# Attention heads every 13 chunks, a lead of two gate pairs, and branch tensors kept in HBM

## The chip, the core and the metric

The kernel runs on one core of a Trainium2 chip. The metric is the device time of one execution in microseconds; lower is better. Three runs of the kernel before gave 492.33, 492.91 and 493.28 us (median 492.91). The engines that matter are TensorE (PE, and PEld for its weight loads), VectorE (DVE), ScalarE (ACT), GpSimd (POOL) and SyncE (SP, which issues most transfers).

## What is computed

One decoder layer on 512 rows of 1024 columns, in float32:

```
h = rmsnorm(x) * norm_g
a_x, a_z, b_q, b_k, b_v, b_z, c_q, c_k, c_v, c_z, gates = split(h @ w_in)
ya = pool_mixer(a_x) * silu(a_z)            # causal windows of 2, 4, 8, 16 rows, then a 128x128 mix per group
yb = sliding_window_attention(b_q, b_k, b_v, sinks) * silu(b_z)    # 8 heads of 64, window 128
yc = block_attention(c_q, c_k, c_v) * silu(c_z)                    # 8 heads of 64
ga, gb, gc = split(sigmoid(gates))
merged = ga * (ya @ w_proj_a) + gb * (yb @ w_proj_b) + gc * (yc @ w_proj_c)
out = rmsnorm(x + merged @ w_out) * final_norm_g
```

At 512 rows the block attention of branch c sees every earlier key, so the kernel computes it as plain causal attention.

## The kernel before

Every matrix product runs on pairs: a float32 tensor is split into a rounded part and the rest (`split`: a ScalarE cast, then a VectorE subtraction), and `mm3` adds three matmuls. Activations are stored with the columns of `h` on the partitions and the 512 rows along the free axis. Weights come from HBM in blocks of 512 KB into five buffers `wr`; `split_cols` (lines 149, 150) casts them on ScalarE to `wh` and subtracts on VectorE to `wl`, four buffers each. `weights(name, ahead)` splits up to three blocks ahead, and each split calls the load of the fourth block behind it.

The program is a sequence of *chunks*, counted by `tick()`: a chunk of the first projections is three matmuls of 512 columns, one of a gate path six of 256. `at(chunk, f)` hangs work of other parts on a chunk. First come 23 units of projections, eight chunks each (`UNITS`), then from chunk 184 the six gate paths `az`, `bz`, `cz` (two pairs each, `PAIRS`), then from chunk 268 the twelve pairs of the merge gates `ga`, `gb`, `gc`, 14 chunks each without their projections, then the output projection with the residual and the final norm.

A pair of gate tiles is computed by `seven` as seven half products instead of eight. It uses three PSUM banks: `pa` takes the first, fourth, sixth and seventh product, so that the ScalarE copies into `sn` (lines 553, 559, 564) must be done before the bank goes on. The part S13 of its weights is loaded by SP (line 135) and added to by an accumulating transfer from POOL (line 137). `between(f)` is called after the third and after the sixth product. There the projection of an earlier pair is put: `project` multiplies the gated branch output `y` with its weights and the gate `sig`, and adds to `m`.

Sixteen attention heads (eight of branch c, then eight of branch b) start at chunk 57, one every 12 chunks. `score` fills a bank, masks on VectorE and takes the exponential on ScalarE; `normalise`, `turn` (transposes to PSUM and splits to `pt`) and `weigh` follow by fixed distances, the last 29 chunks after the head's start. The hi and lo parts of v are side by side, so the result `h.o` holds two partial outputs, on partitions 0 to 63 and 64 to 127. `weigh` copies the second half down with ScalarE (line 510) and adds it on VectorE (line 511) into the tile `ob` or `oc`.

The outputs `oa`, `ob`, `oc` and the gate paths stay in SBUF in tiles of tag `u` (32 units of 4 KB per partition) until `gated(n)` multiplies them and splits the product into `y`. Tag `t2` (four tiles of 2 KB per partition) holds short-lived tensors: `rest`, the pooling chain of `pool_windows`, terms of the merge. All six SiLUs hang on chunk 268 (`silus`, line 343), ordered behind the last exponential; sigmoids are taken in `seven` (line 657).

After the sixth unit the order is no longer the written one. Each engine's queue gets a fixed order by a list scheduler that goes by program order, readiness and free buffers, so work can stand ahead of its place in the code. Once fixed, each engine runs its queue in order.

Of the kernel before, what the change touches and what calls it, by code (L numbers as in the profile page):

```python
# [31 lines left out]

PAIRS = [(n, p) for n in ("az", "bz", "cz") for p in range(2)]

EARLY = 10

START, STEP = 57, 12

# [9 lines left out]
TAIL = 3  # L48

ORDER = (0, 4, 1, 5, 2, 6, 3, 7)  # L50

SUMS = (118,128,138,148)

# [9 lines left out]
def weight_items():  # L63

    def seven(n, p, between=()):
        a, s13, s24, d = (((n, x, p), c) for x, c in (("A", 1024), ("S13", 1024), ("S24", 1024), ("D", 512)))
        return [a, s13, *between, s24, d]

    items = [(u, 1024) for u in UNITS]
    for n, p in PAIRS:  # L70
        items += seven(n, p)
    before = []
    for n in "abc":
        for p in range(4):
            items += seven("g" + n, p, before)
            before = [(("p" + n, p), 1024)]
    return items + before + [(("wo", j), 1024) for j in range(KT)]


@with_exitstack  # L80
def trunk(ctx: ExitStack, tc: tile.TileContext, a, out: bass.AP):
    nc = tc.nc
    pool = ctx.enter_context(tc.tile_pool(name="sb", bufs=1))
    psum = ctx.enter_context(tc.tile_pool(name="ps", bufs=2, space=bass.MemoryType.PSUM))

    def const(name, shape, dt=F32):
        return pool.tile(shape, dt, name=name, tag=name, bufs=1)

    def t2(dt, name):
        return pool.tile([P, S], dt, name=name, tag="t2", bufs=4)  # L90

    def unit(dt, name, shape=(2, S)):

        return pool.tile([P, *shape], dt, name=name, tag="u", bufs=32)
# [204 lines left out]
        hT[k] = hi, lo  # L299


    parts, full, both = {}, {}, {}
    pw = []
    vt = {}

    def kept(kind, i):

        if i % 2 == 0:
            both[kind, i // 2] = unit(F32, f"{kind}{i}")
            full[kind, i], full[kind, i + 1] = both[kind, i // 2][:, 0, :], both[kind, i // 2][:, 1, :]  # L310
        return full[kind, i]

    def evacuate(u, ps):
        kind, i = u
# [23 lines left out]
    def silus():  # L338

        with tc.issue_after(exps[-1].ins):  # L340
            for n, p in PAIRS:
                z = both[n, p]
                nc.scalar.activation(z, z, AF.Silu)

    def keep_v(t, ps):

# [142 lines left out]
    def weigh(s, half):  # L489


        h = head(s)
        if h.moba:
            steps = [(0, 0, 0, 512, 0), (1, 1, 0, 384, 128), (2, 2, 0, 256, 256), (2, 3, 256, 192, 320)]
        else:
            steps = [(0, 0, 0, 256, 0), (0, 2, 256, 256, 256), (1, 1, 0, 256, 128), (1, 3, 256, 192, 320)]
        if h.o is None:
            h.o = bank("PV", f"ps_o{s}")
        for n in (0, 1) if half == 0 else (2, 3):
            b, j, x, w, q0 = steps[n]  # L500
            v = h.v(j)
            for e in range(2):
                nc.tensor.matmul(h.o[:, q0:q0 + w], v, h.pt[b][e][:, x:x + w],  # L503
                                 start=n == 0 and e == 0, stop=n == 3 and e == 1)
        if half == 1:
            kind = "oc" if h.moba else "ob"
            if h.par == 0:
                kept(kind, h.block)
# [69 lines left out]
    def at(chunk, f, *args):  # L578
        todo.setdefault(chunk, []).append((f, args))
# [61 lines left out]
                evacuate(u, ps)  # L641
            tick()
    for n, p in PAIRS:
        kept(n, 2 * p)
        seven(n, p, both[n, p], ("big", "PV", "big"))


    y, merged, ms = {}, {}, {}

    def gated(n):  # L650
        for i in range(4):
            o, z = full["o" + n, i], full[n + "z", i]
            nc.vector.tensor_mul(o, o, z)
            y[n, i] = split(o, f"y{n}{i}")

    def sigmoid(out_, in_, last=False):
        ins = nc.scalar.activation(out_, in_, AF.Sigmoid)
        if last:
            with tc.issue_after(ins.ins):
                nc.scalar.sqrt(one, one)  # L660
# [17 lines left out]
        if n == "c":  # L678
            merged[j] = split(m, f"mg{j}")

    at(268, silus)
    at(268, gated, "a")
    before = None

    def between(f):
        if before:
            project(*before, f)
        if before and f == 1 and before[1] == 1:
            later = {"a": "b", "b": "c"}.get(before[0])
            if later:  # L690
                gated(later)

    for n in "abc":
        for p in range(4):
            sig = unit(F32, f"sig{n}{p}")
            seven("g" + n, p, sig, ("big", "PV", "S"), between, sigmoid)
            before = (n, p, sig)
    between(0)
    between(1)
    assert not todo, sorted(todo)  # L700


# [168 lines left out]
```

## Time and profile before

| | |
|---|---|
| median of three runs | 492.91 us |
| profiled execution | 492.67 us |
| its span, first to last instruction | 490.9 us |
| TensorE, VectorE, ScalarE, GpSimd busy | 476.2, 357.9, 298.0, 48.6 us |
| moved by DMA | 74.19 MB |
| TensorE's clock | 0.993 of full speed on average |

Busy time of TensorE counts matmuls with modelled ends, so a stall shorter than a matmul's pipeline doesn't show as idle time. The stages of the span are: opening to 12 us, first projections to 165.5 us, gate paths to 252.5 us, gate pairs with the branch projections to 429.5 us, output projection to 478.5 us, tail.

### The profile page before, as it was taken

How to read it: one execution, taken by the hardware profiler on the slowest of the kernel's cores; microseconds unless marked ns; L12 is line 12 of the kernel's file. 1: busy time of each engine (PE TensorE's matmuls, PEld its weight loads, DVE VectorE, ACT ScalarE, POOL GpSimd, SP SyncE). 2: the span in 40 equal slices, each digit the busy share in tenths (PEclk: the TensorE clock that was granted, in tenths of full speed). 3: DMA queues.
4: the chain of work that ended last, by engine and by line, in shares of the span. 5: the costliest groups of instructions: out<-in, count | busy, mean ns of one | idle time of the engine just before them, and what ended most of it. 6: DMA issues, size and time to landing. Idle time of an engine off the chain costs nothing.

```text
span 490.9 us, 8122 instructions
## 1 busy us (share of the span) xinstructions
PE 476.2 (97%) x2945; PEld 419.5 (85%) x2945; DVE 357.9 (73%) x676; ACT 298.0 (61%) x596; POOL 48.6 (10%) x90
## 2 busy tenths in 40 slices
PE   8999999999999999999999999999999999999993
PEld 5788888888878889899998999999999999988882
DVE  5559887678997988788899684477856787681255
ACT  6656655587877787866896563445644565551134
POOL 2052000001012200100000000000000000200032
PEclk9999999999999999999999999999999999999997
DMA  8999916827350245554564556644666455590004
GB/s 260 385 244 221 305 50 167 217 89 191 105 127 24 85 105 117 126 150 114 144 152 119 168 142 153 188 123 136 162 166 183 125 154 147 175 354 2 1 1 171
DMA packets 30823, 74.19 MB, mean 151 GB/s; under 512 B 3712, under 2 KB 4736, under 8 KB 30784
## 3 DMA queue, kind: packets, MB, share of 16 engines
q1 hardware_dynamic: 27168, 61.35, 40.4%
q0 software_dynamic: 3472, 12.33, 13.2%
q8 instruction: 23, 0.38, 0.3%
q14 instruction: 16, 0.13, 0.1%
q10 hardware_dynamic: 144, 0.00, 0.0%
HBM read 62.14 MB, written 2.10 MB: 131 GB/s over the span
## 4 chain that ended last, share of the span: by engine, by line
PE 81%; DVE 8%; ACT 5%; DMA 2%; issue 2%; SPq 1%; ACTq 0%; DVEq 0%
PE ps_z L183 2%; PE ps_z L182 2%; PE ps_z L181 2%; PE ps_o L503 2%; ACT wh L149 2%; PE ps_t L475 2%; PE ps_agb L181 2%; PE ps_aga L181 2%; PE acc_bq L181 2%; PE acc_ck L181 2%; PE acc_v L181 2%; PE ps_agb L183 2%; PE acc_v L183 2%; PE ps_agc L183 2%; PE ps_agc L181 2%
## 5 line engine op out<-in xcount | busy, mean ns | idle before, releaser
L149 ACT CAST wh<-wr 128x1024 fp32r<-128x1024 f32 (+2 forms) x120 | 112.7, 943 | 72.8 <-PE ps_z L183 17.2
L150 DVE TENSOR_TENSOR wl<-wr,wh 128x1024 fp32r<-128x1024 f32 (+2 forms) x116 | 126.7, 1097 | 34.6 <-ACT wh L149 33.4
L439 ACT ACTIVATE p<-p,st 128x128 f32<-128x128 f32 (+2 forms) x64 | 33.3, 521 | 20.8 <-DVE st L437 20.7
L137 POOL DMA_DIRECT2D wr<-in_w x18 | 15.5, 863 | 218.9 <-DVE wl L150 87.5
L486 DVE TENSOR_TENSOR pt<-ps_t,pt 128x512 fp32r<-128x512 f32 (+3 forms) x56 | 26.4, 476 | 5.8 <-ACT pt L485 5.6
L485 ACT CAST pt<-ps_t 128x512 fp32r<-128x512 f32 (+3 forms) x56 | 23.0, 416 | 8.0 <-PE ps_t L475 4.0
L182 PE MATMUL ps_z<-wl,mg 128*128 128x512 f32 (+1 forms) x67 | 25.8, 385 | 0.0
L183 PE MATMUL ps_z<-wh,mg 128*128 128x512 f32 (+1 forms) x67 | 25.8, 385 | 0.0
L181 PE MATMUL ps_z<-wh,mg 128*128 128x512 f32 (+1 forms) x67 | 25.8, 385 | 0.0
L475 PE MATMUL ps_t<-ident,p 128*128 128x128 f32 x136 | 21.8, 273 | 0.1
L475 PEld LDWEIGHTS ps_t<-ident,p 128*128 128x128 f32 x136 | 16.1, 140 | 2.5 <-DVE pt L486 0.5
L437 DVE CUSTOM_DVE_ANT_0 p<-ps_s,mask_c,nscale 128x128 f32<-128x128 f32 (+3 forms) x32 | 16.9, 544 | 0.8 <-PE ps_s L431 0.6
L437 DVE CUSTOM_DVE_ANT_0 p<-ps_s,mask_s,nsink 128x256 f32<-128x256 f32 (+1 forms) x32 | 13.9, 443 | 3.4 <-PE ps_s L431 3.2
L453 ACT ACTIVATE p<-p,st 128x256 f32<-128x256 f32 (+3 forms) x32 | 14.4, 515 | 1.9 <-DVE st L448 1.9
L483 POOL MEMSET pt<- 128x64 f32 x32 | 5.1, 234 | 102.3 <-PE ps_o L503 70.4
L182 PEld LDWEIGHTS ps_z<-wl,mg 128*128 128x128 f32 x67 | 12.6, 188 | 2.9
L181 PEld LDWEIGHTS ps_z<-wh,mg 128*128 128x128 f32 x67 | 12.6, 188 | 2.8
L183 PEld LDWEIGHTS ps_z<-wh,mg 128*128 128x128 f32 x67 | 12.6, 188 | 2.8
L503 PEld LDWEIGHTS ps_o<-pt,v 128*128 128x128 f32 x64 | 11.2, 188 | 3.9 <-DVE pt L486 1.1
L503 PE MATMUL ps_o<-pt,v 128*128 128x512 f32 (+3 forms) x64 | 14.0, 325 | 0.4 <-DVE pt L486 0.3
L510 ACT COPY rest<-ps_o 64x512 f32<-64x512 f32 x16 | 9.3, 583 | 6.8 <-PE ps_o L503 5.2
L181 PE MATMUL acc_bq<-hh,wh 128*128 128x512 f32 x32 | 13.4, 418 | 0.0
(439 smaller groups left out, 1644.0 us busy)
## 6 DMA issues: line engine op xcount, KB each, us to landing
wr<-in_w SPq DMA_DIRECT2D x76, 512.0 KB, 4.1
wr<-in_w POOLq DMA_DIRECT2D x18, 512.0 KB, 6.4
wr<-in_w SPq DMA_DIRECT2D x18, 256.0 KB, 3.6
xT<-in_xT SPq DMA_DIRECT2D x8, 256.0 KB, 4.5
xn<-in_x SPq DMA_DIRECT2D x4, 512.0 KB, 9.1
acc<-in_x POOLq DMA_DIRECT2D x4, 512.0 KB, 5.6
out<-yo SPq DMA_DIRECT2D x8, 256.0 KB, 2.3
wr<-in_w SPq DMA_DIRECT2D x8, 128.0 KB, 4.2
```

The lines of the kernel that those rows point to most:

```text
L137: nc.gpsimd.dma_start(t, a["w"][f1 + 1], accum_op=OP.add)
L149: nc.scalar.copy(w_hi[n][:, c], raw_w[n][:, c])
L150: (nc.gpsimd if 4 <= n < 8 else nc.vector).tensor_sub(w_lo[n][:, c], raw_w[n][:, c], w_hi[n][:, c].bitcast(F32))
L181: nc.tensor.matmul(ps, lh, rh, start=start, stop=False, skip_group_check=more)
L182: nc.tensor.matmul(ps, lh, rl, start=False, stop=False, skip_group_check=more)
L183: nc.tensor.matmul(ps, ll, rh, start=False, stop=stop, skip_group_check=more)
L437: nc.vector.tensor_tensor_reduce(out=dst, in0=ps[:, :n], in1=mask, scale=scale, scalar=least, op0=OP.add, op1=OP.min, accum_out=h.st[:, i: ...
L439: exps.append(nc.scalar.activation(dst, dst, AF.Exp, bias=h.st[:, i:i + 1], scale=-1.0, accum_out=h.st[:, 4 + i:5 + i]))
L475: nc.tensor.transpose(ps[:, x:x + P], h.p[:, off:off + P], ident)
L485: nc.scalar.copy(hi[:, c], ps[:, c])
L486: nc.vector.tensor_sub(lo[:, c], ps[:, c], hi[:, c].bitcast(F32))
L503: nc.tensor.matmul(h.o[:, q0:q0 + w], v, h.pt[b][e][:, x:x + w], start=n == 0 and e == 0, stop=n == 3 and e == 1)
```

## The change

A head starts every 13 chunks, so the last one ends at chunk 281, inside the first gate pair. The first projection stands in the third gate pair instead of the second (`LEAD = 2`), and two pairs are projected at the end instead of one. The first two gate pairs use the bank tag `big` where the others use `S`, since the heads still need `S`; the sigmoid of the first pair is put off to chunk 283. The weights are ordered to match.

`weigh` copies both halves of `h.o` to SBUF in one ScalarE copy, stores the first half to a tile in HBM through SP, and lets POOL add the second half to it with an accumulating transfer. `oa` and the six gate paths are stored there too. `back` loads them: those of branch a at chunk 273, those of b and c behind the first projection of the branch ahead. The SiLUs are taken in `gated`, two for each branch, and `gated("a")` moves from chunk 268 to 283.

```
-START, STEP = 57, 12
+START, STEP = 57, 13
+LEAD = 2
+AFTER = 283
...
+    order = [(n, p) for n in "abc" for p in range(4)]
+    proj = [(("p" + n, p), 1024) for n, p in order]
+    for m, (n, p) in enumerate(order):
+        items += seven("g" + n, p, proj[m - LEAD:m - LEAD + 1] if m >= LEAD else ())
+    return items + proj[len(proj) - LEAD:] + [(("wo", j), 1024) for j in range(KT)]
...
+    dram = ctx.enter_context(tc.tile_pool(name="dr", bufs=1, space=bass.MemoryType.DRAM))
...
+    def aside(kind, p):
+        if (kind, p) not in away:
+            away[kind, p] = dram.tile([P, 2, S], F32, name=f"dr{kind}{p}", tag=f"dr{kind}{p}")
+        return away[kind, p]
+    def back(kind):
+        for p in range(2):
+            both[kind, p] = unit(F32, f"{kind}{p}")
+            nc.sync.dma_start(both[kind, p], away[kind, p])
...
-        nc.scalar.activation(kept("oa", i), ps, AF.Copy, scale=psc_sb[:, i:i + 1])
+        o = t2(F32, f"oa{i}")
+        nc.scalar.activation(o, ps, AF.Copy, scale=psc_sb[:, i:i + 1])
+        nc.sync.dma_start(aside("oa", i // 2)[:, i % 2, :], o)
...
-            rest = t2(F32, f"rest{s}")
-            nc.scalar.copy(rest[:HD, :], h.o[HD:, :])
-            nc.vector.tensor_add(full[kind, h.block][h.rows, :], h.o[:HD, :], rest[:HD, :])
+            both_parts = t2(F32, f"op{s}")
+            nc.scalar.copy(both_parts, h.o)
+            o = aside(kind, h.block // 2)[h.rows, h.block % 2, :]
+            nc.sync.dma_start(o, both_parts[:HD, :])
+            nc.gpsimd.dma_start(o, both_parts[HD:, :], accum_op=OP.add)
...
-        seven(n, p, both[n, p], ("big", "PV", "big"))
+        z = unit(F32, f"{n}{p}")
+        seven(n, p, z, ("big", "PV", "big"))
+        nc.sync.dma_start(aside(n, p), z)
...
     def gated(n):
+        with tc.issue_after(exps[-1].ins):
+            for p in range(2):
+                z = both[n + "z", p]
+                nc.scalar.activation(z, z, AF.Silu)
...
-    at(268, silus)
-    at(268, gated, "a")
+    at(AFTER - 10, back, "az")
+    at(AFTER - 10, back, "oa")
+    at(AFTER, gated, "a")
+    at(AFTER, sigmoids)
...
+        if len(waiting) > LEAD:
+            project(*waiting[0], f)
+            if f == 1:
+                n, p, _ = waiting.pop(0)
+                if p == 0 and n != "c":
+                    back("ob" if n == "a" else "oc")
+                    back("bz" if n == "a" else "cz")
+                if p == 1 and n != "c":
+                    gated("b" if n == "a" else "c")
```

## Rows read from the trace of the kernel before

**Rows 1.** The page's first part: busy time, share of the span and instructions of each engine.

```profile
PE 476.2 (97%) x2945; PEld 419.5 (85%) x2945; DVE 357.9 (73%) x676; ACT 298.0 (61%) x596; POOL 48.6 (10%) x90
```

**Rows 2.** The stages of the span: stretch and its length in us, then busy us (and instructions) of PE, PEld, DVE, ACT and POOL, the granted TensorE clock as a share of full speed, the busy share of the DMA engines, GB/s.

```profile
0.00:12.30 12.30, 10.88 (x30) 6.45 (x31) 6.41 (x14) 8.34 (x15) 3.58 (x14) 1.00 0.82 260
12.30:133.00 120.70, 120.64 (x590) 99.90 (x589) 91.46 (x192) 79.03 (x166) 12.78 (x18) 1.00 0.71 201
133.00:165.50 32.50, 32.06 (x162) 25.55 (x161) 29.48 (x67) 24.66 (x58) 5.62 (x13) 1.00 0.24 58
165.50:252.50 87.00, 83.24 (x685) 80.66 (x684) 73.46 (x174) 68.32 (x160) 8.45 (x24) 1.00 0.52 131
252.50:268.00 15.50, 14.99 (x118) 14.25 (x117) 14.82 (x23) 12.87 (x23) 0.86 (x1) 1.00 0.42 123
268.00:429.50 161.50, 161.50 (x1130) 149.68 (x1129) 112.68 (x155) 84.04 (x138) 10.22 (x14) 1.00 0.57 155
429.50:490.90 61.40, 52.85 (x242) 43.03 (x240) 29.61 (x57) 20.75 (x40) 7.12 (x7) 0.95 0.29 106
```

**Rows 3.** The waits of TensorE in the whole span, without those of the opening: tile and line that waited, whom for, us in total, times, longest.

```profile
PE ps_acz L181 <- ACT sncz L564: 0.9, 1, 0.9
PE ps_aaz L181 <- ACT snaz L564: 0.9, 2, 0.5
PE ps_aaz L181 <- ACT snaz L553: 0.7, 1, 0.7
PE ps_aga L181 <- ACT snga L559: 0.5, 1, 0.5
PE ps_abz L181 <- DVE bz L563: 0.4, 1, 0.4
PE ps_abz L181 <- ACT snbz L564: 0.4, 1, 0.4
PE ps_o L503 <- DVE pt L486: 0.3, 1, 0.3
PE ps_dbz L181 <- ACT az L573: 0.3, 1, 0.3
```

**Rows 4.** The timeline of TensorE around one of these stalls: start and duration in us, line, operation, tiles; in brackets the idle time before.

```profile
193.00 0.28 PE L183 MATMUL ps_abz<-hh,wl 128*128 128x256 f32 x1
193.12 0.28 PE L181 MATMUL ps_abz<-hh,wh 128*128 128x256 f32 x1
193.88 0.39 PE L181 MATMUL ps_aaz<-hh,wh 128*128 128x256 f32 x1 [0.48 <-ACT snaz L564]
194.10 0.28 PE L182 MATMUL ps_aaz<-hl,wh 128*128 128x256 f32 x1
```

**Rows 5.** The timeline of ScalarE ahead of another one, in which TensorE waited for the last row's copy.

```profile
177.12 1.04 ACT L149 CAST wh<-wr 128x1024 fp32r<-128x1024 f32 x1
...
178.25 1.04 ACT L149 CAST wh<-wr 128x1024 fp32r<-128x1024 f32 x1
179.20 0.37 ACT L564 COPY snaz<-ps_aaz 128x256 f32<-128x256 f32 x1
```

**Rows 6.** The instructions on the tile `rest`: line, engine, operation, count, shortest, median and longest ns, first and last start.

```profile
L510 ACT COPY rest<-ps_o x16: 582/583/586, 74.1 to 257.7; 64x512 f32<-64x512 f32 x16
L511 DVE TENSOR_TENSOR oc<-ps_o,rest x8: 673/683/685, 74.7 to 162.9; 64x512 f32<-64x512 f32 x8
```

**Rows 7.** ScalarE's groups by shape from 165 to 252.5 us: busy us, mean ns, idle before. Of the head's groups (lines 439, 442, 453, 485, 510, ten in all) the first, a middle one and the last.

```profile
L439 ACT ACTIVATE p<-p,st 128x256 f32<-128x256 f32 x18 | 9.1, 508 | 1.5 <-DVE st L437 1.4
...
L485 ACT CAST pt<-ps_t 128x512 fp32r<-128x512 f32 x7 | 4.1, 586 | 0.3
...
L453 ACT ACTIVATE p<-p,st 128x128 f32<-128x128 f32 x3 | 1.2, 401 | 1.9 <-DVE st L448 1.9
```

**Rows 8.** The SiLUs of line 343 (those of `bz` lie between), in the columns of rows 6, and last a row of ScalarE's timeline that lies among them in time.

```profile
L343 ACT ACTIVATE az<-az x2: 1062/1068/1073, 242.1 to 244.5; 128x1024 f32<-128x1024 f32 x2
...
L343 ACT ACTIVATE cz<-cz x2: 1066/1076/1085, 251.0 to 253.4; 128x1024 f32<-128x1024 f32 x2
L343 ACT ACT_TABLE_LOAD  x1: 1283/1283/1283, 240.8 to 240.8; - x1
...
249.49 0.38 ACT L564 COPY sncz<-ps_acz 128x256 f32<-128x256 f32 x1
```

**Rows 9.** ScalarE in the first gate pair, 252.5 to 268 us: two groups by shape, then two rows of the sigmoids' line in the columns of rows 6.

```profile
L149 ACT CAST wh<-wr 128x1024 fp32r<-128x1024 f32 x4 | 4.2, 1052 | 0.4 <-PE ps_bga L182 0.4
L175 ACT CAST ya<-oa 128x512 fp32r<-128x512 f32 x4 | 2.4, 621 | 0.0
...
L657 ACT ACTIVATE siga<-siga x2: 422/534/647, 257.3 to 265.2; 128x256 f32<-128x256 f32 x1, 128x512 f32<-128x512 f32 x1
...
L657 ACT ACTIVATE siga<-ps_aga x1: 383/383/383, 264.7 to 264.7; 128x256 f32<-128x256 f32 x1
```

**Rows 10.** Transfers: the issue of one accumulating load on POOL and VectorE's first use of it; the times to landing of the accumulating loads from 160 to 270 us, and those of the four transfers of 128 KB into `bk0his`.

```profile
189.03 0.85 POOL L137 DMA_DIRECT2D wr<-in_w  x1 [7.44 <-DMA wr<-in_w]
...
204.64 0.68 DVE L161 TENSOR_TENSOR wr<-wr,wr 128x512 f32<-128x512 f32 x1
...
DMA to landing us min/median/max: 5.1/5.4/5.6
...
DMA to landing us min/median/max: 2.2/2.3/2.4
```

More of the change, by code (lines that the diff above doesn't have):

```diff
@@ L71, in weight_items @@
         items += seven(n, p)
[L72 to L77, printed above, removed]
+    order = [(n, p) for n in "abc" for p in range(4)]
[3 more added lines that the diff above has]
+    return items + proj[len(proj) - LEAD:] + [(("wo", j), 1024) for j in range(KT)]
 @with_exitstack
@@ L299, in normed_rest @@
         hT[k] = hi, lo
-    parts, full, both = {}, {}, {}
+    parts, full, both, away = {}, {}, {}, {}
     pw = []
     vt = {}
[L306 to L311, printed above, removed]
+    def aside(kind, p):
[6 more added lines that the diff above has]
+            nc.sync.dma_start(both[kind, p], away[kind, p])
     def evacuate(u, ps):
@@ L336, in evacuate @@
                 pool_windows(i)
[L338 to L343, printed above, removed]
     def keep_v(t, ps):
@@ L506, in weigh @@
             kind = "oc" if h.moba else "ob"
-            if h.par == 0:
-                kept(kind, h.block)
-            rest = t2(F32, f"rest{s}")
-            nc.scalar.copy(rest[:HD, :], h.o[HD:, :])
-            nc.vector.tensor_add(full[kind, h.block][h.rows, :], h.o[:HD, :], rest[:HD, :])
+            both_parts = t2(F32, f"op{s}")
[3 more added lines that the diff above has]
+            nc.gpsimd.dma_start(o, both_parts[HD:, :], accum_op=OP.add)
     sums = {}
@@ L643, in trunk @@
     for n, p in PAIRS:
-        kept(n, 2 * p)
-        seven(n, p, both[n, p], ("big", "PV", "big"))
+        z = unit(F32, f"{n}{p}")
+        seven(n, p, z, ("big", "PV", "big"))
+        nc.sync.dma_start(aside(n, p), z)
     y, merged, ms = {}, {}, {}
     def gated(n):
+        with tc.issue_after(exps[-1].ins):
+            for p in range(2):
+                z = both[n + "z", p]
+                nc.scalar.activation(z, z, AF.Silu)
         for i in range(4):
-            o, z = full["o" + n, i], full[n + "z", i]
+            o, z = (both[kind, i // 2][:, i % 2, :] for kind in ("o" + n, n + "z"))
             nc.vector.tensor_mul(o, o, z)
@@ L679, in project, with sigmoids @@
             merged[j] = split(m, f"mg{j}")
-    at(268, silus)
-    at(268, gated, "a")
-    before = None
-    def between(f):
[L686 to L699, printed above, removed]
+    def sigmoids():
+        with tc.issue_after(exps[-1].ins):
+            for sig in early:
+                sigmoid(sig, sig)
+    early = []
+    at(AFTER - 10, back, "az")
+    at(AFTER - 10, back, "oa")
+    at(AFTER, gated, "a")
+    at(AFTER, sigmoids)
+    waiting = []
+    def between(f):
+        if len(waiting) > LEAD:
[7 more added lines that the diff above has]
+                    gated("b" if n == "a" else "c")
+    for m, (n, p) in enumerate((n, p) for n in "abc" for p in range(4)):
+        sig = unit(F32, f"sig{n}{p}")
+        if m < LEAD - 1:
+            early.append(sig)
+        waiting.append((n, p, sig))
+        seven("g" + n, p, sig, ("big", "PV", "big" if m < LEAD else "S"), between, None if m < LEAD - 1 else sigmoid)
+    while waiting:
+        n, p, sig = waiting.pop(0)
+        for f in range(2):
+            project(n, p, sig, f)
     assert not todo, sorted(todo)
```

## The prediction

> **What bounds the kernel now.** I read the page's busy lines first [rows 1]: TensorE is busy 97% of a 490.9 us span, so work taken from other engines pays only where TensorE waits for it. The table by stages [rows 2] tells where that is. Each line is one stretch: opening, first projections, their last part, the six plain gate paths beside the heads of branch b, the first gate pair, the other gate pairs with the branch projections, output projection and tail. From 12.3 to 133 us TensorE loses 0.06 us, from 268 to 429.5 us nothing. The first and the last stretch lose 1.4 and 8.6 us in work that the diff leaves as it is. What is left lies in three stretches: 0.44, 3.76 and 0.51 us, 4.7 us in all.
>
> The waits of TensorE [rows 3] name them: nine stalls, 4.4 us. Seven wait for a ScalarE copy (the lines of `sn`, of `az`), two for VectorE. A marked stall costs more than its mark. In the row of one [rows 4] matmuls of 256 columns start 0.12 us apart; across the stall the starts are 0.76 us apart, 0.64 more than the step, with 0.48 marked; the next step is 0.22, another 0.10. So each stall costs its mark and 0.26 us, and the nine cost 4.4 + 9 x 0.26 = 6.7 us. That is all that better order can win here, since the change keeps every matmul.
>
> Why the copies are late shows before one of them [rows 5]: ScalarE runs two casts of 1.04 us ahead of the `sn` copy at 179.20, one of the two for which `ps_aaz` waits 0.9 us [rows 3]. `seven` puts its sixth product into the bank of `pa` and its seventh into the same bank, so the copy between them has no cover but what lies beside it: heads, or a projection at `between(1)`. That is why the stretch with projections loses nothing. ScalarE is busy 79% in the gate paths (68.3 of 87.0) and VectorE 84% (73.5 of 87.0); from 133 to 165.5 us VectorE has 29.5 of 32.5 [rows 2].
>
> **The change part by part.** The sum is made on the profiled execution: 492.67 us, of which 490.9 are span. It lies 0.24 us under the median of 492.91, within the spread of the three runs.
>
> *Heads every 13 chunks, without the VectorE addition.* Per head the change drops a VectorE add of 0.68 us [rows 6]. ScalarE's copy grows from 64 to 128 partitions with the same 512 columns; the cast of `pt` on 128 partitions takes 0.586 us beside 0.583 us [rows 6, 7], so it costs nothing more. From 133 to 165.5 us three adds (2.0 us) go and the head work thins by 1/13, so VectorE falls to about 27 of 32.5 us. The one stall there, 0.3 + 0.26, I count as gone: -0.6. Bounds: 0 to -0.6.
>
> *The gate paths, 165.5 to 252.5 us.* VectorE loses seven adds (4.8 us). On ScalarE five SiLUs at 1.07 us and their table load of 1.28 us [rows 8] move out of this stretch, 6.6 us. The ten groups of the heads come to 36 us, from 9.1 down to 1.2 [rows 7], and 1/13 of that is 2.8. That leaves about 59 of 87, 68% instead of 79%. Seven of the nine stalls are here (3.6 us marked). The longest, 0.9 us, is for the `sncz` copy at 249.49, which lies among the SiLUs [rows 8]; it goes with them: 0.9 + 0.26 = 1.16. The other six cost 2.7 + 6 x 0.26 = 4.3 us. They come from casts and copies that become ready at the same moment, and that remains; I take a third off, 1.4. Together -2.6. Bounds: 0 to -5.5.
>
> *Two gate pairs without a projection.* Today the first gate pair alone has no projection beside it, and it keeps one stall of 0.5 + 0.26 = 0.77 us [rows 3]. With `LEAD = 2` the second is bare too, so I add 0.77 for it. The first keeps the last head's turns and weighing as cover. But the second holds `gated("a")` and `sigmoids`. ScalarE's work in it, from the first pair's rows [rows 8, 9]: weights 3.5 casts of 1.05, 3.7, the four copies of `seven` at 0.37 [rows 5] 1.5, its own sigmoids 0.65 + 0.42 + 0.38 = 1.45, two SiLUs 2.2, four casts of `ya` 2.5, two table loads 2.6, and the sigmoid of 1024 columns put off from the first pair, about 1.1 like a SiLU of that size: 15 us. TensorE has 84 matmuls of 0.117 us there [rows 4], 9.8 us. So 5 us are too many unless they move. The first pair has room: 3.7 + 1.5 and some 1.6 for the rest of a head (two casts and a copy like those of rows 7) make 6.8, beside at least 9.8 us of TensorE. And today the SiLUs run from 242 us, ten microseconds ahead of their place in the code, chunk 268 at about 252.5 us [rows 8]; y of branch a is needed only in the third pair. I take 0.4 of extra stall: +1.2 together. Bounds: 0 to +5.2.
>
> *Tables.* SiLU of b and c now stands between sigmoids: two more changes there and back, four loads of 1.28 us. ScalarE is busy 84 of 161.5 us there [rows 2] and projections cover the banks; 0. Without cover one load would be one stall: at most 4 x 1.3 us.
>
> *New transfers.* SP gets 38: sixteen halves of heads (128 KB), four of `oa`, six gate paths of 512 KB, twelve loads of 512 KB. POOL gets sixteen accumulations. What is behind them on both queues are weight loads; the accumulating part of S13 is the last to arrive. One such is issued at 189.03 us, lands after 5.4 us, and is first used at 204.64, 10 us of cover [rows 10]. A head's accumulation holds POOL until the SP half has landed, 2.3 us for 128 KB [rows 10], and for 0.85 us of issue: 3.2 us, inside 10. Also behind it on POOL is the next head's fill of the gap in `pt`, due five chunks later, some 4 us, and read six chunks after that. The twelve loads come in three lots of 2 MB; the gate pairs run their DMA engines at 0.57 with 155 GB/s [rows 2], so a lot of 2 MB takes some 7 us of them, and it is needed more than a gate pair later. I put 0 for all. Bounds: below, 0, since none of TensorE's waits [rows 3] is for a transfer that could come earlier; above, where the cover fails, the excess of one S13, 3.2 us, once or twice.
>
> *SBUF.* Twelve units leave for HBM. No wait in rows 3 is for a unit, so that itself gives nothing. But `op` and `oa` now take one of the four `t2` slots until their transfers are done (rival C).
>
> Sum: -0.6 - 2.6 + 1.2 = -2.0 us: 490.7 us.
>
> **Rivals.** *A, the stalls are structural.* The thinner heads leave the six copies late as they are; only the SiLU stall and the one at 146 us go, and the second bare pair gives that back: -0.6 - 1.16 + 1.5 = -0.3, 492.4 us, no change. For: casts and copies become ready together whatever the heads do, and a new order makes new meetings. Against: 11 points less load on ScalarE.
>
> *B, slower: the second gate pair is bound by ScalarE.* If `gated("a")` and its tables don't move ahead of it, TensorE waits there for the 5.2 us that the copies are late: 492.67 - 3.2 + 5.2 = 494.7 us. It decides from where the SiLUs of `az` start: before the second gate pair has begun, it fails. For: their input now comes back from HBM, called ten chunks ahead, so they can't run ten microseconds early as today unless SP issues the loads early. Against: SP is idle most of the time and the slots are free.
>
> *C, slower: `t2`.* `rest` holds a slot for 0.58 + 0.68 = 1.3 us [rows 6]; `op` for 0.58 + 2.3 + 0.85 + 5.4 = 9.1 us [rows 6, 10] of a head's 12.5 (seven heads in the 87 us of the gate paths). `pool_windows` holds three of the four at once, and `oa` a fourth. If VectorE, at 91% from 133 to 165.5 us, waits in its order for a transfer, say 1.5 us in each of four groups, it is 6 us: 492.67 - 2 + 6 = 496.7 us. Against: a group lasts about 4 us of each ten, and the queues' order is made with the slots in view.
>
> On this the Trainium skill (SBUF — State Buffer, section "SBUF: two separate sides") has a rule that speaks against the change: a DMA issued from GpSimd waits for its descriptors while VectorE runs an operation that takes both ports, so accumulations beside a busy VectorE would land late. Here the accumulating loads land in 5.1 to 5.6 us beside a VectorE that is busy 84% [rows 2, 10], a narrow spread, so nothing as strong is seen; by the rule `op` would hold its slot longer, and rival C would weigh more.
>
> *D, more.* Nearly all stalls up to 252.5 us go, the bare pairs cost 0.8: 492.67 - 0.6 - 4.6 + 0.8 = 488.3 us.
>
> **How the numbers follow.** Forecast 0.38, A 0.22, B 0.15, C 0.10, D 0.15. A change under 0.2%, 1 us, can't be told from none here: faster 0.38 + 0.15 = 0.53, within 0.22, slower 0.25. The likeliest case is 490.7, by itself 489.3 to 491.8. The range takes D in and B, and leaves out most of C and the far end of D: 488.0 to 494.8 us.
>
> **What would show it.** The waits of TensorE: the 0.9 us stall at the last gate path gone, fewer marks from 165 to 260 us, one or two new ones in the first two gate pairs. From 133 to 165.5 us VectorE under 28 us per 32.5. SiLUs of `az` before the second gate pair begins (else B). No wait of VectorE or TensorE for an `op` or `oa` transfer (else C). No wait for `wr` by ScalarE that passes on to TensorE. The stretch with projections still without idle. It is wrong if the stalls from 165 us to the third gate pair sum to 4.7 us marked or more.

## The result, and the profile after

The change makes the kernel slower: 498.01 us median of five runs (496.22 to 500.45) against 493.21 us of the kernel before on the same chip, a ratio of 1.011 (95% interval 1.007 to 1.015). The forecast was 490.7 us, with a range to 494.8 us. The profiled execution took 496.22 us, the shortest of the five.

One number ahead of the prediction is wrong: there are 22 units of projections, not 23. So the gate paths begin at chunk 176 and the gate pairs at chunk 260. After the change the last head ends in the second gate pair, not in the first. Chunk 268, which the prediction puts at 252.5 us, began at 256.7 us before the change, so the SiLUs ran some 14 us ahead of it, not ten.

The page's busy times, as in [rows 1]:

```profile
PE 476.2 (96%) x2945; PEld 419.3 (85%) x2945; DVE 350.5 (71%) x660; ACT 305.8 (62%) x603; POOL 62.1 (13%) x106
```

TensorE's work is the same 476.2 us, so all that was lost is idle time. The table of stages, in the columns and stretches of [rows 2]; the last two rows part the end differently:

```profile
0.00:12.30 12.30, 10.83 (x32) 6.29 (x33) 6.81 (x15) 8.60 (x16) 3.60 (x14) 1.00 0.83 256
12.30:133.00 120.70, 120.48 (x583) 99.18 (x582) 88.78 (x180) 76.26 (x156) 16.77 (x21) 1.00 0.75 212
133.00:165.50 32.50, 32.39 (x176) 27.14 (x175) 29.14 (x69) 25.00 (x61) 7.14 (x17) 1.00 0.44 110
165.50:252.50 87.00, 83.47 (x689) 80.97 (x689) 67.48 (x165) 63.28 (x159) 14.34 (x29) 1.00 0.74 193
252.50:268.00 15.50, 13.99 (x114) 13.38 (x114) 9.87 (x15) 11.28 (x19) 1.96 (x4) 1.00 0.85 258
268.00:429.50 161.50, 159.24 (x1113) 147.20 (x1112) 116.05 (x162) 100.20 (x155) 11.92 (x16) 1.00 0.64 184
429.50:470.00 40.50, 40.50 (x175) 32.62 (x174) 18.47 (x22) 11.79 (x15) 0.00 (x0) 1.00 0.27 100
470.00:495.00 25.00, 15.26 (x75) 12.53 (x73) 13.87 (x38) 9.41 (x26) 6.40 (x5) 0.90 0.23 85
```

The stretches are the same in time, not quite in work: the first matmul of `ga` starts at 244.4 us, before the change at 247.5. Length less PE's busy time is TensorE's idle time. Against [rows 2] it changes by -0.33 us from 133 to 165.5 us, by -0.23 in the gate paths, by +1.00 from 252.5 to 268, by +2.26 in the other gate pairs and by +0.2 in the two stretches before 133 us. The span after 429.5 us holds 0.6 more (64.9 - 55.76 against 61.4 - 52.85). That is 3.5 us, the difference of the two spans (494.4 and 490.9). So nearly all of it is lost in the gate pairs, which lost 0.51 us before and 3.77 now. The gate paths, from which the forecast took its gain, give almost nothing. From 252.5 to 268 us the DMA engines are now at 0.85 with 258 GB/s, where they were at 0.42 with 123.

The waits of TensorE, in the columns of [rows 3]:

```profile
PE ps_agb L186 <- ACT sngb L568: 1.5, 1, 1.5
PE ps_aaz L186 <- ACT snaz L568: 1.4, 2, 0.7
PE ps_o L507 <- ACT pt L489: 1.3, 1, 1.3
...
PE ps_abz L186 <- ACT snbz L568: 1.0, 2, 0.5
PE ps_aaz L186 <- ACT snaz L557: 1.0, 1, 1.0
```

The 0.9 us for `sncz` is gone. The waits for `snaz` grew (1.4 and 1.0, before 0.9 and 0.7), those for `snbz` too. New are 1.3 us for a cast of `pt` and 1.5 us for `sngb`. What stood ahead of these two shows in ScalarE's timeline, first at 258 us, then at 316 us (start, duration, line, operation; in brackets the idle time before, and what ended it):

```profile
258.19 1.28 ACT L659 ACT_TABLE_LOAD   x1
262.17 1.06 ACT L659 ACTIVATE az<-az 128x1024 f32<-128x1024 f32 x1 [2.69 <-DMA az<-draz]
263.13 0.25 ACT L489 CAST pt<-ps_t 128x128 fp32r<-128x128 f32 x1
...
316.80 1.05 ACT L154 CAST wh<-wr 128x1024 fp32r<-128x1024 f32 x1 [3.32 <-DMA wr<-in_w]
317.75 0.37 ACT L568 COPY sngb<-ps_agb 128x256 f32<-128x256 f32 x1
```

Both waits have one form. ScalarE runs its queue in order and stands at an instruction whose transfer hasn't landed: first the load of `az` from HBM, later a weight. The small copy for which TensorE waits is queued behind it: 2.69 us of standing became 1.28 us of stall, 3.32 became 1.51. The weight was an S13 part. SP loads its first half, and POOL's accumulating load follows, here issued at 308.59:

```profile
308.59 0.87 POOL L142 DMA_DIRECT2D wr<-in_w  x1 [15.41 <-DVE wl L155]
```

That load landed after 8.1 us, no longer than such loads took before the change (below). It was late because it was sent late: 4.4 us after ScalarE's first copy of the pair then under way (304.15), where the kernel before has 1.2 us (311.20 and 310.05). SP had stood at the first half until VectorE gave a weight buffer free, and the DMA engines were nearly idle meanwhile. A wait of SP's queue, and a stretch in the columns of [rows 2]:

```profile
SPq L140 <- DVE wl L155: 9.1, 1, 9.1
...
300.00:304.00 4.00, 4.00 (x31) 3.77 (x30) 4.00 (x7) 2.59 (x5) 0.00 (x0) 1.00 0.01 4
```

No load of a branch was under way then; SP had issued the last one of branch b at 287.14. But VectorE's splits `yb` of branch b ran until 304.0 us, right up to this pair; before the change they ended at 287.9, 22 us ahead of the same pair. So this stall comes from a buffer that was free late, not from a slow transfer. That the late work of branch b held the buffer is likely, but not shown apart.

All accumulating loads of that line from 268 to 430 us: who waited for them in all, and issue to landing:

```profile
ACT wh L154: 6.0, 4
DVE wr L166: 2.4, 2
...
DMA to landing us min/median/max: 5.2/7.8/9.5
```

The same view of the kernel before, which the prediction doesn't use:

```profile
ACT wh L149: 1.8, 1
DVE wr L161: 0.5, 1
...
DMA to landing us min/median/max: 7.2/7.8/8.4
```

There they took 7.2 to 8.4 us already, against the 5.1 to 5.6 of [rows 10], and ScalarE stood 1.8 us and VectorE 0.5 us for one of them: the cover in the gate pairs was used up in places, though no stall of TensorE came of it. After the change the median is the same; the longest, 9.5 us, was issued at 338.14 beside the loads of `oc`.

### The profile page after: what moved, and what is told of

Same layout as the page of the kernel before. It is cut to its first block, busy times and chain, and to the rows that moved or that the text cites. A ratio compares the mean times of both kernels' runs of the same rounds, so it can differ in the third digit from the quotient of the medians.

```text
span 494.4 us, 8248 instructions
## 1 busy us (share of the span) xinstructions
PE 476.2 (96%) x2945; PEld 419.3 (85%) x2945; DVE 350.5 (71%) x660; ACT 305.8 (62%) x603; POOL 62.1 (13%) x106
## 3 DMA queue, kind: packets, MB, share of 16 engines
q1 hardware_dynamic: 31616, 73.94, 46.8%
## 4 chain that ended last, share of the span: by engine, by line
PE 45%; DVE 8%; ACT 7%; DMA 5%; issue 3%; SPq 0%; POOL 0%; ACTq 0%; DVEq 0%; POOLq 0%
ACT wh L154 3%; PE ps_z L188 2%; PE ps_z L187 2%; PE ps_z L186 2%; DMA wr<-in_w 2%; DVE wl L155 2%; DMA cz<-drcz 2%; PE ps_agc L188 2%; PE ps_agc L187 2%; PE ps_agc L186 2%; PE ps_pc L188 2%; PE ps_pc L186 2%; PE ps_pc L187 2%; DMA az<-draz 1%; PE ps_pa L187 1%
## 5 line engine op out<-in xcount | busy, mean ns | idle before, releaser
L515 POOL DMA_DIRECT2D droc<-op x8 | 6.7, 832 | 79.3 <-DMA droc<-op 34.6
L515 POOL DMA_DIRECT2D drob<-op x8 | 6.7, 837 | 61.8 <-DMA drob<-op 22.1
L166 DVE TENSOR_TENSOR wr<-wr,wr 128x512 f32<-128x512 f32 x18 | 12.4, 687 | 2.6 <-DMA wr<-in_w 2.4
```

## The experiments

Theory T: the cost is the twelve loads back from HBM, through engines that stand at a late transfer. Some expectations part it: T1, the waits for these loads themselves; T2, the weight blocks that they push back. Rivals: the SiLU table loads (S); the order that comes with the new spacing and lead (G); the heads' accumulations on POOL. Each ratio is to the kernel before, run on the same chip. Every edit makes the order of the queues anew, so two runs can differ in more than the edited line.

**The changed kernel once more**, unedited:

> The changed kernel as it is, to see how far one profile stands for the others. Its five runs lie from 496.2 to 500.5 us, against 492.3 to 493.6 before. Theory T (transfers): ScalarE's queue stands at an instruction that waits for a transfer (a SiLU for its load from HBM, a cast for its weight block), and the copies for TensorE behind it are late; how late differs from run to run, so another profile shows the same kind of stall at other places and sizes, 3 to 8 us more than before in all. Theory S (tables): the stalls sit at the same instructions with the same sizes within 0.2 us, behind table loads. Theory G (order): the marked stalls of TensorE from 165 to 260 us make up the difference.

499.1 us, 1.013 (1.011 to 1.016). The profiled execution is longer than the one above by 4.6 us of span, and shows how the time spreads from run to run. VectorE's timeline first:

```profile
269.16 1.29 DVE L662 TENSOR_TENSOR oa<-oa,az 128x512 f32<-128x512 f32 x2 [3.85 <-DMA oa<-droa]
```

Then windows of 1 us, in the columns of [rows 2]:

```profile
272.00:273.00 1.00, 0.83 (x6) 0.83 (x7) 1.00 (x3) 1.00 (x3) 0.00 (x0) 0.85 0.08 33
273.00:274.00 1.00, 1.00 (x6) 1.00 (x6) 1.00 (x2) 0.98 (x3) 0.00 (x0) 0.50 0.03 12
274.00:275.00 1.00, 1.00 (x7) 1.00 (x6) 1.00 (x2) 1.00 (x1) 0.51 (x1) 0.50 0.00 0
275.00:276.00 1.00, 1.00 (x7) 1.00 (x7) 1.00 (x2) 0.99 (x2) 0.31 (x1) 0.50 0.18 39
276.00:277.00 1.00, 1.00 (x10) 1.00 (x10) 1.00 (x3) 0.96 (x3) 0.00 (x0) 0.94 0.88 199
```

And TensorE's timeline:

```profile
272.17 0.39 PE L186 MATMUL ps_aga<-hh,wh 128*128 128x256 f32 x1 [2.38 <-DVE siga L567]
...
273.61 0.41 PE L188 MATMUL ps_aga<-hh,wl 128*128 128x256 f32 x1
273.82 0.41 PE L186 MATMUL ps_aga<-hh,wh 128*128 128x256 f32 x1
```

VectorE stood 3.85 us for a load of `oa`, TensorE stalled 2.38 us, and then its granted clock was 0.50 (1.2 of 2.4 GHz) for about 3 us. Matmuls that step 0.12 us in [rows 4] step 0.21 there. The clock's rows add up to 1.7 us lost: one stall of 2.4 us costs about 4.

**No loads.** The twelve loads are left out; a GpSimd memset fills the tiles at the same place.

```
-            nc.sync.dma_start(both[kind, p], away[kind, p])
+            nc.gpsimd.memset(both[kind, p], 0.5)
```

> The twelve loads of `back` are left out: GpSimd fills their tiles with 0.5 instead, so the products of the branches use constants; the stores to HBM stay. Theory T: most of the loss goes, 491 to 494 us. Theories S and G: no change against the changed kernel, 496 to 500 us.

491.61 us, 0.997 (0.996 to 0.998). All of the loss goes. The order is another too: ScalarE's table loads in the gate pairs fall from ten to six. The new heads, the lead and the stores with their accumulations are worth -1.3 us together, where the forecast had -2.0 for the whole change. In its table of stages the loss in the gate paths stays (87.00 - 83.41), that from 252.5 to 268 us goes, and 1.4 us stay in the last row:

```profile
165.50:252.50 87.00, 83.41 (x689) 80.86 (x688) 67.74 (x165) 63.04 (x159) 14.89 (x30) 1.00 0.73 192
252.50:268.00 15.50, 15.48 (x132) 15.27 (x131) 11.87 (x18) 13.56 (x23) 5.61 (x8) 1.00 0.66 165
268.00:429.50 161.50, 160.12 (x1112) 148.18 (x1111) 116.88 (x162) 96.18 (x151) 19.27 (x24) 1.00 0.59 161
```

This execution was the longest of its ten (492.93 us), so it doesn't show where the 1.3 us come from.

**Bytes without waits.** Each load goes from HBM to HBM instead; nothing waits for it, and it holds no tile.

```
-            nc.sync.dma_start(both[kind, p], away[kind, p])
+            nc.gpsimd.memset(both[kind, p], 0.5)
+            nc.sync.dma_start(dram.tile([P, 2, S], F32, name=f"cp{kind}{p}", tag=f"cp{kind}{p}"), away[kind, p])
```

> The twelve loads of 512 KB become copies from HBM to HBM, issued at the same places; no SBUF tile and no instruction waits for them, the branches use tiles filled with 0.5. So it has the traffic of the loads (more of it: the copies are written to HBM) without their waits and without their tiles. If the loss is the weight blocks that the traffic pushes back: 496 to 500 us. If it is the waits for the loads themselves, or the tiles: 491 to 493, as without the loads (491.6).

494.42 us, 1.002 (1.001 to 1.003), 2.8 us over the kernel without loads. But that isn't the price of the traffic in the gate pairs. With no tile to wait for, the list scheduler moved the copies far ahead. One group of their issues, then the same group in the changed kernel (count, ns of issue, first and last start in us):

```profile
L321 SPq DMA_DIRECT2D cpoc<-droc x2: 497/512/527, 121.5 to 175.9; - x2
...
L320 SPq DMA_DIRECT2D oc<-droc x2: 423/530/637, 338.1 to 341.3; - x2
```

Eleven of the twelve copies were issued before 256 us, the last at 273.7. So the run shows neither answer that was expected of it: what the bytes cost where the loads stand, it doesn't tell.

**Waits without bytes.** The loads keep place, tile and waits but carry 32 of 512 columns.

```
-            nc.sync.dma_start(both[kind, p], away[kind, p])
+            nc.gpsimd.memset(both[kind, p], 0.5)
+            nc.sync.dma_start(both[kind, p][:, :, :32], away[kind, p][:, :, :32])
```

> The twelve loads from HBM keep their place, tiles and waits but carry 32 of 512 columns; the other columns are 0.5 from a GpSimd memset, so the SiLUs and products have other data. If the 2 MB lots cost by their bytes (weights and the loads themselves landing late), nearly all of the loss goes: 491.5 to 493 us. If the loss is in instructions that stand at a load in a queue's order, and in the tiles that are held from the call on, it stays above 495 us.

496.01 us, 1.007 (1.004 to 1.009), 4.4 us over the kernel without loads, with a sixteenth of the bytes. That was the answer expected of waits and tiles. ScalarE at 350 us:

```profile
349.45 1.28 ACT L660 ACT_TABLE_LOAD   x1 [1.85 <-DMA cz<-drcz]
350.75 1.06 ACT L660 ACTIVATE cz<-cz 128x1024 f32<-128x1024 f32 x1
351.71 1.98 ACT L154 CAST wh<-wr 128x1024 fp32r<-128x1024 f32 x2
353.60 0.36 ACT L569 COPY sngb<-ps_agb 128x256 f32<-128x256 f32 x1
```

The load of `cz`, called behind its memset and landing a median 5.0 us later though it has only 32 KB, holds ScalarE for 1.85 us. Then table, SiLU and two casts run ahead of `sngb`, and TensorE waits 1.77 us for it, its longest stall. The changed kernel is 6.4 to 7.5 us over the one without loads. So most of that, 4.4 us, stays with a sixteenth of the bytes, and 2.0 to 3.1 us go with the rest. Two limits: these loads start behind the memset, later than in the changed kernel (the first of `az` at 259.8 us instead of 255.3), and their short rows aren't free. By the pages' shares of SP's DMA queue (43.9% of 491.2 us without loads, 44.2% of 496.2 here, 46.8% of 494.4 in the changed kernel) they held the DMA engines for an estimated 3.7 us, the full loads for 15.8.

**Loads that nobody reads**, into twelve other tiles, while the branches use tiles filled with 0.5:

```
-            nc.sync.dma_start(both[kind, p], away[kind, p])
+            nc.gpsimd.memset(both[kind, p], 0.5)
+            nc.sync.dma_start(unit(F32, f"un{kind}{p}"), away[kind, p])
```

> The twelve loads of `back` run as before, but into tiles that nothing reads; the branches use tiles that GpSimd fills with 0.5. It leaves the traffic and takes away every wait for it by SiLU and product. Theory T1 (the loss is the wait of SiLU and product for their own loads): 491 to 493 us, as without the loads (491.6). Theory T2 (the loss is the weight blocks that the loads push back): 496 to 499 us. Both halves: 493.5 to 495.5.

498.04 us, 1.010 (1.007 to 1.013), no gain. This doesn't separate what it was made for: the doubled tiles wait for each other, SP stands up to 8.2 us at a load for a tile whose own earlier load is still under way, and ScalarE 3.2 us for one. It shows that tiles of tag `u` are scarce here.

**Loads called earlier.** First those of branch a ten chunks earlier, then all twelve one by one, spread out:

```
-    at(AFTER - 10, back, "az")
-    at(AFTER - 10, back, "oa")
+    at(AFTER - 20, back, "az")
+    at(AFTER - 20, back, "oa")
...
+BACK = ((260, "oa", 0), (263, "oa", 1), (266, "az", 0), (269, "az", 1), (294, "ob", 0), (300, "bz", 0), (306, "ob", 1), (312, "bz", 1), (382, "oc", 0), (388, "cz", 0), (394, "oc", 1), (400, "cz", 1))
...
+    for c, kind, p in BACK:
+        at(c, back, kind, p)
```

> Only the four loads of branch a are called ten chunks earlier (263 instead of 273), so that they land before the SiLUs and products want them. T1: 2 to 4 us better than the changed kernel (495 to 497 beside 498 to 499), the stall of the second gate pair gone; the stalls from 300 us on stay. T2: no change, 498 to 500.

> The loads of branch a earlier still (chunks 260 to 269), and those of b and c one by one, six chunks apart, instead of four at a time. The bytes are the same. T1 and T2 alike: most of the loss goes, 491.5 to 494. If the loss hangs on the bytes and not on when they are asked for: 496 or more.

501.46 us (1.014 to 1.019) and 506.07 us (1.022 to 1.032): both worse, the first beyond either theory's answer. With the earlier call the order is made anew, and the reader moves forward with its load. In the first the SiLU of `az` comes at 255.0 us instead of 262.2, stands 1.0 us for its load all the same, and VectorE stands 3.8 us for that SiLU. In the second, SP's queue stands 9.9 us at a load that waits for its tile, weight loads stand behind it, and ScalarE stands 8.4 us for weights (6.0 in the changed kernel). The first's wait, then two of the second:

```profile
DVE oa L662 <- ACT az L659: 3.8, 1, 3.8
...
SPq L321 <- DVE oc L663: 9.9, 1, 9.9
...
ACT wh L156 <- DMA wr<-in_w: 8.4, 4, 3.5
```

**Rivals.** Four edits: SiLU computed as sigmoid, so that no table changes; heads every 12 chunks again; heads every 12 and lead and places as before, which leaves the HBM part alone; the halves of a head added on VectorE again and stored by one transfer, without POOL's accumulations.

```
-            nc.scalar.activation(z, z, AF.Silu)
+            nc.scalar.activation(z, z, AF.Sigmoid)
...
-START, STEP = 57, 13
+START, STEP = 57, 12
...
-LEAD = 2
+LEAD = 1
-AFTER = 283
+AFTER = 270
...
-            nc.gpsimd.dma_start(o, both_parts[HD:, :], accum_op=OP.add)
+            nc.vector.tensor_add(rest[:HD, :], h.o[:HD, :], rest[:HD, :])
...
```

> The SiLU of the gate paths is computed as a plain sigmoid (the multiplication by z is left out), so ScalarE needs no table change among the gates. Theory S: the loss shrinks to under 1.5 us, 492 to 494.5. Theory T: ScalarE still waits at the same instructions for their transfers; at most 1.5 us better than the changed kernel, 495 to 499.

> The changed kernel with the heads every 12 chunks; all else as in the change. It tells what the thinner heads themselves are worth. The transfers' theory: 497 to 501, the same stalls behind the loads, as the loads of branch a stand where they did. If the thinner heads give what was forecast for them (some 2 us less stall from 133 to 252 us): 1.5 to 2.5 us slower than the changed kernel. If they give nothing: within 1 us of it.

> All transfers of the change, with the heads every 12 chunks and a lead of one gate pair as before (first load at chunk 260, `gated(a)` at 270). Theory T: as slow as the changed kernel or slower, 495 to 501 us, since the first projection comes a gate pair earlier and its inputs are due sooner. Theory G: near the kernel before, 492 to 494.

> The two halves of a head are added on VectorE as before and stored by one DMA, so the sixteen accumulations on POOL go and the loads from HBM stay. If the accumulations hold POOL's queue, and S13's accumulations behind them, to the cost of the stalls up to 252 us, it gains about 1 us, 496 to 497 us. If these stalls are ScalarE's order, it stays at 498 us or goes up with VectorE's seven adds of 0.68 us in the gate paths.

Tables: 498.19 us, 1.012 (1.008 to 1.016), no different from the changed kernel, so they cost nothing that shows. Heads every 12: 500.79 us, 1.015 (1.012 to 1.018); the thinner heads may be worth a microsecond or two, but the intervals overlap. HBM alone: 509.75 us, 1.034 (1.031 to 1.037); with a lead of one pair ScalarE stands 4.7 us at the SiLU of `az` and TensorE 5.3 us behind it. The run with heads every 12 differs from it only in the lead of two and the later places, so these hide some 9 us of what the loads cost. Addition on VectorE: 499.55 us, 1.014 (1.010 to 1.018), no gain; the accumulations aren't the cause. No rival gives back what leaving out the loads does.

**More weight buffers.** If late weights are the loss, one more buffer should hide them. Six and seven buffers, each taking a tile of tag `u`; the control is the kernel before with six:

```
-        raw_w[n] = pool.tile([P, 1024], F32, name=f"wr{n}", tag="wr", bufs=5)
+        raw_w[n] = pool.tile([P, 1024], F32, name=f"wr{n}", tag="wr", bufs=6)
-            load_upto(m + 4)
+            load_upto(m + 5)
...
```

> The changed kernel with six weight buffers `wr` instead of five, loads called five blocks ahead instead of four, and one tile of tag `u` less to make room (31). If late weight blocks are the loss, a block more of lead, some 3 us, takes a good part of it: 493 to 496 us. If the waits for the branch loads are: no change, 498 to 500.

> The same with seven weight buffers, loads six blocks ahead, and 30 tiles `u`. Late weights: 491.5 to 494.5 us, less than with six. Waits for the branch loads: 498 or more. If the missing tiles bind: slower than with six.

> The kernel before with six weight buffers and 31 tiles `u`, as a control. Its weight blocks land in time, so no gain: 492.5 to 494 us; or slower, if the tile that it gives up binds, since it keeps its branch tensors in SBUF.

496.41 us (1.004 to 1.008), 505.79 us (1.022 to 1.030) and 498.08 us (1.007 to 1.013). Then six with all 32 tiles, the broadcast of rstd put into one of them, in both kernels; last, in the changed kernel, with the earlier calls only from the gate pairs on:

```
-    rstd_bc = const("rstd_bc", [P, S])
+    rstd_bc = unit(F32, "rstd_bc")[:, 0, :]
...
-            load_upto(m + 4)
+            load_upto(m + (5 if m >= index[("ga", "A", 0)] else 4))
```

> A sixth buffer for raw weights, loads called one item earlier, and all 32 tiles of tag u: the broadcast of rstd, dead after the opening, moves into one of these tiles to make room. If what the loads from HBM cost is late weights (ScalarE's casts standing in order at a weight that shares the DMA engines with 2 MB of loads), and the 496.4 us with six buffers and 31 tiles kept only the price of the missing tile (3.2 us of stall at 146 us and the slower clock after it), this gives 491 to 493 us and no stall of over 1 us anywhere from 133 to 430 us. If the tiles that wait for loads are the limit by themselves, it stays at 495 us or more.

> The same sixth buffer and the same place for the broadcast of rstd in the kernel before, nothing of the change: the control. Its stalls are ScalarE's order in the gate paths, not weights: if so, 492 to 494 us, no change. If the sixth buffer helps any kernel, it is below 491.5 us, and its gain in the changed kernel is not about the loads from HBM.

> The changed kernel with a sixth buffer for raw weights and all 32 tiles (the broadcast of rstd in one of them), but loads called one item earlier only from the first gate pair on. In the run with the earlier calls everywhere VectorE stood 2.7 us at the move of bq3 near 140 us, because SP had stood at an earlier weight load, and that run lost nothing from 274 us on. If the late weights cost the changed kernel what it loses in the gate pairs, and the earlier calls cost the rest, both go here: 491.5 to 493.5 us, no stall of over 1.3 us, gate pairs full. If the sixth buffer only moves the loss, 495 us or more.

496.08 us (1.004 to 1.011), 495.76 us (1.004 to 1.008) and 495.83 us (1.005 to 1.011). The control lies outside both of its answers: the sixth buffer makes the kernel before slower by 3 us even with its tiles. The two others come out at 495 us or more, and later calls don't help. But with the sixth buffer the changed kernel is no slower than its control. The last kernel's stages in its shortest execution, and below them a row of VectorE's timeline, show both sides:

```profile
252.50:268.00 15.50, 15.47 (x133) 15.27 (x132) 10.66 (x19) 12.12 (x19) 1.95 (x4) 1.00 0.99 309
268.00:429.50 161.50, 161.39 (x1129) 149.35 (x1128) 118.54 (x165) 100.13 (x158) 11.92 (x16) 1.00 0.66 190
```

```profile
140.24 0.69 DVE L527 TENSOR_TENSOR s<-r 128x512 f32<-128x512 f32 x1 [2.43 <-DMA bq3two<-bq]
```

The gate pairs are full again, with the DMA engines at 0.99 in the first of the two stretches. The first six-buffer kernel, profiled in an execution at its median, has 161.19 us of the 161.50 too. So a block more of lead for the weights takes nearly all of the loss in the gate pairs, with the same loads still there. But at 140 us VectorE stands 2.43 us for a move of `bq3` (0.3 in the changed kernel), and TensorE stalls 2.27 us at 147 us. In the control it is the same move, here in VectorE's waits:

```profile
DVE s L523 <- DMA bq3two<-bq: 2.0, 1, 2.0
```

The list scheduler goes by free buffers, so a sixth one gives SP another order everywhere, whatever the calls say: ahead of the move SP is one weight load further on (at 132.13 us it sends a part D, where the changed kernel sends an S13), and issuing the four transfers of the move takes 3.81 us instead of 2.69. The shortest of the last kernel's nine executions took 493.61 us, the longest 500.12, with mean granted clocks of 0.995 and 0.986.

**Nothing in HBM.** The same heads, lead and SiLUs, with all branch tensors in 33 tiles and the halves added on VectorE:

```
-    rstd_bc = const("rstd_bc", [P, S])
+    rstd_bc = unit(F32, "rstd_bc")[:, 0, :]
-        return pool.tile([P, *shape], dt, name=name, tag="u", bufs=32)
+        return pool.tile([P, *shape], dt, name=name, tag="u", bufs=33)
...
-        if (kind, p) not in away:
-            away[kind, p] = dram.tile([P, 2, S], F32, name=f"dr{kind}{p}", tag=f"dr{kind}{p}")
-        return away[kind, p]
+        if (kind, p) not in both:
+            both[kind, p] = unit(F32, f"{kind}{p}")
+        return both[kind, p]
...
```

> The changed kernel's schedule (heads every 13 chunks, two gate pairs ahead, SiLUs in the gate pairs) with nothing in HBM: the gate paths and head outputs stay in tiles of tag u and VectorE adds the halves as before; 33 tiles, the broadcast of rstd in one of them. If the loss is the way through HBM alone, the thinner heads give 490 to 492.5 us. If the tiles are what binds, the heads and gates stand at tiles and it is 495 us or more, with waits for tiles of sig, T or r on VectorE and ScalarE.

493.83 us, 1.001 (1.000 to 1.002), between the two answers. The loss is the way through HBM: without it 4 to 5 us come back (with one tile of tag `u` more than the changed kernel has). But the schedule gains nothing by itself. One of its twelve executions, the profiled one, took 1203.11 us, with TensorE's matmuls at about twice their usual time; why isn't known, and where the expected gain stays can't be read from it. No version that computes the whole result beat the kernel before.

## Why the prediction was wrong

*The step that failed: "I put 0 for all"* of the new transfers, with a bound of "the excess of one S13, 3.2 us, once or twice". The runs put 6.4 to 7.5 us on the twelve loads. Three things were wrong in that step. The prediction's own sign of being wrong was met too: the marked stalls from 165 us to the third gate pair sum to 4.9 us.

First, the cover. The 10 us of [rows 10] are from the gate paths. All three lots of 2 MB go to the gate pairs (from 255, 280 and 338 us), where the trace of before had accumulating loads of 7.2 to 8.4 us and waits of 1.8 and 0.5 us for one of them. I worked the lot's cost out as "some 7 us" of DMA engines and didn't set it against the weights that share them. In the changed kernel the first lot held the DMA engines at a share of 1.06 and 376 GB/s from 262 to 266 us, and loads of `az` took a median 7.1, of `oa` 8.5 and of `cz` 9.3 us. The Trainium skill (DMA: Bandwidth & Descriptors, section "Issuing engines are not separate DMA queues") says that transfers from all issuing engines interleave on the same 16 DMA engines; POOL's S13 load of 9.5 us, issued beside SP's loads of `oc`, agrees. By the fit on the same page (section "Anatomy of one DMA — SWDGE (gpsimd) path"), which is for transfers issued by GpSimd, 512 KB alone would be an estimated 3.2 us. GpSimd's accumulating loads of 512 KB took 5.2 to 9.5 us in the gate pairs, and the measured times decide. The six-buffer kernels point to the weights' lead as the cover that was missing: with a block more of it the gate pairs are nearly full beside the same loads, though in another order.

Second, "it is needed more than a gate pair later" counted from the call in the code, and for branch a it doesn't hold even there: `back` stands at chunk 273 and `gated` at 283, ten chunks, where a bare pair has 14. The list scheduler seems to have put the SiLU of `az` right behind the time it expected the load to land. Its table load ran at 258.19, when the load had been issued 2.9 us before; SP issued the two halves of `az` at 255.28 and 257.58. The order was fixed beforehand, and on the chip ScalarE stood in it.

Third, I priced a late transfer by who reads it. The price is what stands behind the reader in its queue. With a sixteenth of the bytes 4.4 of the 6.4 to 7.5 us stayed, in such waits and in tiles held for the loads. The stall at 316 us shows how far it reaches: no branch load was under way, and a weight was late because its buffer was.

*From 133 to 165.5 us, -0.6*: TensorE's idle time fell by 0.33 us, within the bounds. The reason given isn't borne out: VectorE has 29.14 us, not under 28.

*The gate paths, -2.6*: idle time fell by 0.23. The SiLU stall went as forecast, but the "third off" the others (1.4) didn't come; the waits for `snaz` and `snbz` grew by 1.4 us in all (from 1.6 to 2.4 and from 0.4 to 1.0), which is more than the SiLU's stall had cost. ScalarE is at 73% (63.28 of 87.0), not 68%. Here rival A was right: the stalls are structural. Without the loads they stay as they are (3.59 us idle).

*The bare gate pairs, +1.2*: from 252.5 to 268 us the loss grew by 1.0, but by the late load of `az`, not by crowded SiLUs; that the size nearly fits is luck. By the prediction's sign it was rival B: the SiLUs of `az` ran at 262.17 and 269.50 us, and the second gate pair had begun by 257 us. Rival B also named the loads as what speaks for it. Its mechanism, ScalarE bound by work, isn't what is seen: the stall came with ScalarE idle for 2.69 us.

*Tables, 0*: the price was right, the count wasn't. There are eight table loads more than before, not four, as the SiLUs of a branch run apart with sigmoids between. *Rival C*, `t2`: no wait of TensorE or VectorE for a transfer of `op` or `oa` to HBM shows in the changed kernel.

*The sum without the loads*: -1.3 us (0.2 to 0.4%) against -2.0. The mechanism for that part is not confirmed: with everything in SBUF the same schedule gives +0.1%. What stays open is whether the 1.3 us come from the adds that VectorE loses or from the tiles that become free, how the 4.4 us divide between instructions that stand in a queue and tiles that are held, and what the bytes alone cost in the gate pairs.

## What to carry to other kernels

A transfer that is added to a stretch is priced there: against the landing times and first uses of the transfers that already run in that stretch, not against the slack in another. On an engine that runs its queue in order, look at what is queued behind the instruction that reads a load; it stalls too, though it has nothing to do with the load. A transfer that nothing waits for may not stay where the code calls it: see in the trace where it ran before reading a price from it. One more buffer can move a stall out of one stretch and into another, when the order of the queues is made anew around it; try it on the kernel before as well.

## Unexpected on the chip

After a stall of 2.4 us TensorE's granted clock was at half for about 3 us, and matmuls of 256 columns stepped 0.21 us instead of 0.12. The kernels here with such stalls spread more: the changed kernel's five runs lie within 4.2 us and the last six-buffer kernel's nine within 6.5, the longer of these at the lower mean clock (0.986 to 0.992 against 0.994 and 0.995), while the kernel without loads has ten within 2.0.

Loads of 32 KB in rows of 128 bytes took a median 5.0 us (`cz`) and 6.0 us (`oc`) from issue to landing, no less than the 512 KB weights around them (4.6 us).
